# Issuing the stores of a softmax-gradient kernel from Pool in place of ACT

## The chip, the core and the metric

The kernel runs on one core of a Trainium2 chip. A core has a matrix engine (PE), a vector engine (DVE), a scalar engine (ACT), GpSimd (Pool) and a sync engine (SP), each with its own queue of instructions, and 16 DMA engines that all queues share. The metric is the device time of one execution in microseconds, as the median of several runs.

## What is computed

For each of 8 x 1024 = 8192 rows of 8192 float32 logits the kernel computes the softmax and subtracts one at the row's label. 268 MB come in and 268 MB go out.

```python
logits_max = np.max(logits, axis=-1, keepdims=True)
exp_logits = np.exp(logits - logits_max)
softmax = exp_logits / np.sum(exp_logits, axis=-1, keepdims=True)
...
one_hot[batch_idx, seq_idx, labels] = 1.0
return (softmax - one_hot).astype(np.float32)
```

## The kernel before

The 8192 rows are cut into 64 tiles of 128 rows (one row in each partition, 32 KB of it). Two tiles form a group, so there are 32 groups; within a group each partition holds two neighbouring rows, 64 KB. SBUF has three slots (`SLOTS`) of one group each, `X`, and everything is done in place in them: a tile is loaded into its slot, turned into its gradient there, and stored from there.

The order is written out by hand. `run` appends an instruction to an engine's queue, with the semaphore values it has to wait for, and returns the semaphore value that it will reach. Because every instruction is recorded in that helper, nearly all have line 68 in the profile, and the waits that are split off from them line 67.

- `load(b)` issues the loads of group `b` on SP. The string `LOADS` says how: "r" as two DMAs of one tile (4 MB), "w" as one DMA of both tiles (8 MB). A load into a slot that was used before waits for the stores from that slot to land (`put` semaphores). There are 43 loads: 22 of one tile, 21 of two.
- `row_max(t)` lets DVE take the negated maximum of each row of tile `t` into `m`; it waits for the load (`got` semaphores).
- ACT computes the exponential in place, with the row sum in `s`. DVE computes `r`, its reciprocal. ACT scales the row by `r`, in place. DVE subtracts one at the label: it compares an index row `iota`, which lies in PSUM as int16, with the label, and subtracts.
- `store(t)` issues the store of tile `t` (4 MB), after DVE's last step on that tile (`finished[t]`). All 64 stores are of this kind.

In the loop over tiles, DVE's queue holds the reciprocal of tile `t`, then the maximum of tile `t + 1`, then the subtraction of tile `t`. ACT's queue holds the exponential of tile `t`, then the store of tile `t - 1`, then the scaling of tile `t`. For the last tile the scaling and the subtraction are done in two halves. At the end, ACT waits for the stores of the last three groups. Pool only prepares: an identity matrix, and the index row, which it writes into the third slot before that is loaded.

Of the kernel before, what the change touches and what calls it, by code (L numbers as in the profile page):

```python
# [9 lines left out]
SLOTS = 3  # L10
# [7 lines left out]
def kernel(  # L18
# [6 lines left out]
    nc = tc.nc  # L25
# [30 lines left out]
    with tc.tile_critical():  # L56
        sem = tc.alloc_semaphore
        got = [[sem(f"got{i}{q}") for q in range(2)] for i in range(SLOTS)]
        put = [[sem(f"put{i}{q}") for q in range(2)] for i in range(SLOTS)]
# [3 lines left out]
        def run(engine, waits, counter, method, **operands):  # L63

            waits = list(dict.fromkeys(waits))
            for w in waits[:-1]:
                engine.wait_ge(*w)
            instruction = getattr(engine, method)(**operands)  # L68
            for w in waits[-1:]:
                instruction._wait_ge(*w)  # L70
            step = 16 if method == "dma_start" else 1
            instruction.then_inc(counter, step)
            count[counter.name] = count.get(counter.name, 0) + step
            return counter, count[counter.name]
# [3 lines left out]
        w = run(nc.gpsimd, [], pool, "memset", ap=ident[:], constant=0.0)  # L78
# [13 lines left out]
        for j in range(G):  # L92
            w = run(
                nc.tensor, [w_ident, w_lab], pe, "transpose",
                out=lab_ps[:, j, :], in_=lab_f[:, j, :], identity=ident[:],
            )
# [20 lines left out]
        loaded, stored, finished = {}, {}, []  # L117
# [14 lines left out]
        def store(t):  # L132
            b, j = divmod(t, G)
            stored.setdefault(b, [])
            for q, piece in enumerate(PIECES[STORES[b]]):
                ps, js = piece
                if js.stop != j + 1:
                    continue
                w = run(
                    nc.scalar, [finished[t]], put[b % SLOTS][q], "dma_start",  # L140
                    out=o_b[b, ps, js, :], in_=X[ps, b % SLOTS, js, :],
                )
                stored[b].append((piece, w))
# [16 lines left out]
        for t in range(T):  # L160
            x = row(t)
            label = lab[:, t % G, t // G : t // G + 1]
            w = run(
                nc.scalar, [w_max], act, "activation",
                out=x, in_=x, func=Act.Exp, bias=m[:, t : t + 1], scale=1.0, accum_out=s[:, t : t + 1],
            )
# [5 lines left out]
            if t > 0:  # L172
                store(t - 1)
# [10 lines left out]
            for c, w in zip(cols, scaled):  # L184
                w = run(
                    nc.vector, [w], dve, "scalar_tensor_tensor",
                    out=x[:, c], in0=iota[:, c], scalar=label, in1=x[:, c],
                    op0=Alu.is_equal, op1=Alu.subtract, reverse1=True,
                )
            finished.append(w)  # L190
        store(T - 1)
        for b in range(B - SLOTS, B):
            for _, w in stored[b]:
                nc.scalar.wait_ge(*w)


# [28 lines left out]
```

## Time and profile before

| what | value |
|---|---|
| time, median of 3 runs | 1247.4 us (1247.38 to 1247.5) |
| span of the profiled execution | 1245.7 us, 592 instructions |
| DVE, ACT, Pool busy | 1119.2, 919.1, 7.4 us |
| loads (SP's queue, q1) | 6192 packets, 268.44 MB |
| stores and the labels (ACT's queue, q10) | 9264 packets, 268.51 MB |
| mean DMA rate over the span | 431 GB/s |

The times come from the page of one profiled execution, the first row from the timed runs; of the profiled execution the page gives the span, from the first to the last instruction, which leaves out the start and end of the launch around it. A packet is one contiguous piece that a DMA engine moves; the last piece of each DMA on each engine is a mark of 4 bytes that raises the semaphore, which is why the queues have 16 small packets for each DMA besides their data. The queue q10 also carries the labels.

### The profile page before, as it was taken

The page shows a single profiled execution, that of the slowest core. Times are in us where ns is not written, and L with a number is a line of the kernel's source. Part 1 is how long each engine was busy: PE and PEld are TensorE (multiplying, and loading weights), DVE is VectorE, ACT ScalarE, POOL GpSimd, SP SyncE. Part 2 cuts the span into 40 slices and gives each one's busy share as a digit, 9 for nine tenths or more (in the row PEclk, how much of TensorE's full clock was granted, in tenths as well). Part 3 has the DMA queues.
Part 4 walks back from the last instruction along what each step waited for, and adds up shares of the span by engine and source line. Part 5 has one row for each costly group of instructions (what it writes and reads, how often), then busy time and mean ns, then how long its engine had stood idle before and what let it go on. Part 6 is the DMA issues. An engine that isn't in the chain of part 4 may idle for free.

```text
span 1245.7 us, 592 instructions
## 1 busy us (share of the span) xinstructions
PE 0.4 (0%) x2; PEld 0.3 (0%) x2; DVE 1119.2 (90%) x196; ACT 919.1 (74%) x194; POOL 7.4 (1%) x7
## 2 busy tenths in 40 slices
PE   0000000000000000000000000000000000000000
PEld 0000000000000000000000000000000000000000
DVE  5999998888988889888998888988889999999893
ACT  3888886778776787767877778777777788887772
POOL 2000000000000000000000000000000000000000
DMA  9999999999999999999999999999999999999998
GB/s 406 417 429 433 438 433 442 437 426 427 430 435 445 439 417 442 426 430 437 432 443 438 420 435 432 430 437 450 420 426 437 436 428 432 437 435 429 432 437 386
DMA packets 15460, 536.98 MB, mean 431 GB/s; under 512 B 1728, under 2 KB 1728, under 8 KB 1760
## 3 DMA queue, kind: packets, MB, share of 16 engines
q1 hardware_dynamic: 6192, 268.44, 50.0%
q10 hardware_dynamic: 9264, 268.51, 49.9%
q14 instruction: 4, 0.03, 0.0%
HBM read 268.50 MB, written 268.44 MB: 431 GB/s over the span
## 4 chain that ended last, share of the span: by engine, by line
DMA 59%; DVE 37%; another core or an unknown queue 2%; ACT 1%; DVEq 0%; issue 0%; PE 0%; SPq 0%; ACTq 0%
DMA X<-in_logits_dram 31%; DMA out_dram<-X 27%; DVE m L68 18%; DVE X L68 18%; ACT X L68 1%; DVE iota L68 0%; DVEq L56 0%; DMA lab_raw<-in_labels_dram 0%; DVE lab_f L68 0%; DVE r L68 0%; PE iota L68 0%; SPq L68 0%; ACTq L68 0%; DVE lab L68 0%
## 5 line engine op out<-in xcount | busy, mean ns | idle before, releaser
L68 DVE TENSOR_REDUCE m<-X 128x1 f32<-128x8192 f32 x64 | 555.2, 8675 | 94.3 <-DMA X<-in_logits_dram 94.3
L68 ACT ACTIVATE X<-X,m 128x8192 f32<-128x8192 f32 x64 | 455.9, 7123 | 188.4 <-DVE m L68 188.4
L68 DVE SCALAR_TENSOR_TENSOR X<-iota,lab,X 128x8192 f32<-128x8192 int16 (+1 forms) x65 | 559.7, 8612 | 4.1 <-ACT X L68 4.1
L68 ACT ACTIVATE X<-X,r 128x8192 f32<-128x8192 f32 (+1 forms) x65 | 456.0, 7017 | 115.9 <-DVE r L68 115.9
L68 DVE RECIPROCAL r<-s 128x1 f32<-128x1 f32 x64 | 9.9, 154 | 7.3 <-ACT X L68 7.3
L68 ACT ACTIVATION_READ_ACCUMULATOR X<-X,m 128x1 f32 x64 | 12.0, 187 | 0.0
L68 DVE CAST lab_f<-lab_raw 32x256 f32<-32x256 int32 x1 | 3.7, 3685 | 4.7 <-DMA lab_raw<-in_labels_dram 4.7
L68 POOL IOTA X<- 128x8192 int16 x1 | 6.9, 6944 | 0.0
L68 DVE TENSOR_SCALAR iota<-X 128x4096 int32<-128x4096 int32 x1 | 4.4, 4427 | 0.1
L68 ACT ACT_TABLE_LOAD x1 | 1.3, 1283 | 1.3 <-SPq L56 1.3
L68 DVE COPY lab<-iota 128x64 f32<-128x64 f32 x1 | 0.2, 225 | 0.5 <-PE iota L68 0.5
L68 PE MATMUL iota<-ident,lab_f 32*128 32x32 f32 x2 | 0.4, 300 | 8.5 <-DVE lab_f L68 8.5
L68 PEld LDWEIGHTS iota<-ident,lab_f 32*128 32x128 f32 x2 | 0.3, 196 | 8.4 <-DVE lab_f L68 8.4
L68 POOL TENSOR_SCALAR_AFFINE_SELECT ident<-ident 32x32 f32<-32x32 f32 x1 | 0.2, 204 | 0.1
L68 POOL MEMSET ident<- 32x32 f32 x1 | 0.1, 115 | 0.5 <-SPq L56 0.5
L209 POOL MEMSET const-bfloat16-1.0<- 128x1 bf16 x1 | 0.1, 107 | 0.0
L209 POOL MEMSET const-uint8-127<- 128x1 uint8 x1 | 0.1, 107 | 0.0
L209 POOL MEMSET const-float32-0.0<- 128x1 f32 x1 | 0.1, 104 | 0.2 <-issue 0.2
L209 POOL MEMSET const-float32-1.0<- 128x1 f32 x1 | 0.1, 104 | 0.0
## 6 DMA issues: line engine op xcount, KB each, us to landing
out_dram<-X ACTq DMA_DIRECT2D x64, 4096.0 KB, 30.8
X<-in_logits_dram SPq DMA_DIRECT2D x22, 4096.0 KB, 26.6
X<-in_logits_dram SPq DMA_DIRECT2D x21, 33.4
lab_raw<-in_labels_dram ACTq DMA_DIRECT2D x1, 64.0 KB, 3.8
```

The costliest lines, as they stand in the source:

```text
L68: instruction = getattr(engine, method)(**operands)
L209: nc = _bacc.Bacc("TRN2", target_bir_lowering=False, num_devices=1)
```

## The change

The 64 stores are issued from Pool's queue. The waits at the end of the program for the last six of them move with them. What each store waits for, what it moves, and their order among themselves stay as they are, and so do all loads and all compute instructions.

```diff
@@ -137,7 +137,7 @@
                 if js.stop != j + 1:
                     continue
                 w = run(
-                    nc.scalar, [finished[t]], put[b % SLOTS][q], "dma_start",
+                    nc.gpsimd, [finished[t]], put[b % SLOTS][q], "dma_start",
                     out=o_b[b, ps, js, :], in_=X[ps, b % SLOTS, js, :],
                 )
                 stored[b].append((piece, w))
@@ -191,7 +191,7 @@
         store(T - 1)
         for b in range(B - SLOTS, B):
             for _, w in stored[b]:
-                nc.scalar.wait_ge(*w)
+                nc.gpsimd.wait_ge(*w)
```

## The prediction

> **What bounds the kernel now.** I read the page's busy shares first, then its slices and DMA queues, then windows, waits and the last microseconds.
>
> ```profile
> span 1245.7 us, 592 instructions
> PE 0.4 (0%) x2; PEld 0.3 (0%) x2; DVE 1119.2 (90%) x196; ACT 919.1 (74%) x194; POOL 7.4 (1%) x7
> ...
> DMA  9999999999999999999999999999999999999998
> ...
> q1 hardware_dynamic: 6192, 268.44, 50.0%
> q10 hardware_dynamic: 9264, 268.51, 49.9%
> ```
>
> No compute engine is full: DVE 90%, ACT 74%, Pool almost empty. The DMA row is 9 in all slices but the last, and the two queues (q1: loads from SP, q10: stores from ACT) together fill 99.9% of the 16 DMA engines' time. A digit 9 could still hide 10% of idle time; the windows say it doesn't (the last two columns are DMA share and GB/s):
>
> ```profile
> 200.00:600.00 400.00, 0.00 (x0) 0.00 (x0) 358.66 (x64) 295.26 (x63) 0.00 (x0) 1.00 1.00 434
> 600.00:1000.00 400.00, 0.00 (x0) 0.00 (x0) 361.30 (x62) 299.66 (x63) 0.00 (x0) 1.00 1.00 433
> ...
> 1235.00:1240.00 5.00, 0.00 (x0) 0.00 (x0) 0.00 (x0) 0.00 (x0) 0.00 (x0) 1.00 0.99 426
> 1240.00:1245.70 5.70, 0.00 (x0) 0.00 (x0) 0.00 (x0) 0.00 (x0) 0.00 (x0) 1.00 0.41 178
> ```
>
> The share is 1.00 until about 1240 us. So the time is the sum of the packets' times on an engine. In the trace's records of single packets, one of 32,768 bytes takes 1.213 us and one of 65,536 bytes 2.418 us, nearly without spread. Per engine: stores 512 x 1.213 = 621 us; loads 168 x 2.418 + 176 x 1.22 (the first ones are slower) = 621 us; in all 1242 us. The engines start about 2 us into the span, the last store lands at 1244.15, and the waits and barriers behind it take 1.55 us.
>
> ```profile
> SPq L68 <- DMA out_dram<-X: 699.1, 37, 57.3
> SPq L67 <- DMA out_dram<-X: 446.9, 21, 21.5
> ...
> ACT X L68 <- DVE m L68: 188.4, 64, 19.7
> ...
> DVE m L68 <- DMA X<-in_logits_dram: 94.3, 25, 6.9
> ```
>
> These waits show who feeds whom: SP's loads wait for stores to land and free a slot, DVE's row maximum waits for loads, ACT for DVE. They alternate in the chain of waits too, which makes store latency look critical. But a 4 MB store lands a median 30.8 us after its issue only because it shares full engines with a load. What counts is whether the engines ever run dry. From issues and packet ends I added up the bytes issued but not moved: at the issue of each of the first 62 stores at least 8.4 us of work (at 431 GB/s) is still queued, at the 63rd 7.1 us, and at the last 3.6 us.
>
> ```profile
> 1217.03 0.15 DVE L68 RECIPROCAL r<-s 128x1 f32<-128x1 f32 x1
> 1217.14 0.34 ACTq L68 DMA_DIRECT2D out_dram<-X  x1
> 1217.53 7.31 ACT L68 ACTIVATE X<-X,r 128x4096 f32<-128x4096 f32 x2 [1.83 <-DVE r L68]
> 1221.27 8.88 DVE L68 SCALAR_TENSOR_TENSOR X<-iota,lab,X 128x4096 f32<-128x4096 int16 x2 [4.09 <-ACT X L68]
> 1230.18 0.34 ACTq L68 DMA_DIRECT2D out_dram<-X  x1
> ```
>
> This timeline is the end: row 62's store, row 63's scaling and subtraction, and the last store, issued 13.9 us before it lands.
>
> **The change part by part.** *ACT loses 64 issues of 338 ns, 21.6 us.* Each stands between two ACTIVATEs and starts when DVE has finished the row before. Without it the scaling ACTIVATE starts about 0.35 us earlier, but DVE's next step on that row waits for its own 8.68 us row maximum, against 7.12 us of scaling: 1.2 us of cover that was there already. Only for row 63 there is no maximum to hide behind, and there the last store could be issued 0.3 us earlier; queued packets cover that. Worth 0 us. ACT's waits on the last stores also leave; nothing is queued behind them but the end.
>
> *Pool gains 64 stores, each behind a wait for DVE's subtraction.* What is queued behind a waiting store on Pool is only the next store; Pool's 6.94 us index row ends at 8.3 us, and the first store is due at 47 us. Each store waits for the same DVE step as before, and in the same order, so SP's loads and the slots keep their releases. Loads stay on SP.
>
> *Start of a store.* No row shows Pool issuing a DMA. Below, it could be as quick as ACT's 0.34 us. Above, I use the whole trip of a small transfer on idle engines, the label load: 3.78 us from issue to landing; a path slower by that much again starts each store 3.8 us later. For 63 stores the queued work (7.1 us and more) covers both ends: 0. For the last store 3.6 us is queued on average, but the engines' end marks lie 2.1 us apart, so the emptiest has about 2.4 us: between 0 and 1.4 us exposed. I take 0.5.
>
> *The packets themselves.* The bytes and rows are the same; whether a packet from Pool's queue costs what one from ACT's does, the trace cannot show. The fixed part of a packet is 2 x 1213 - 2418 = 8 ns; shedding it wholly saves 512 x 8 = 4.1 us per engine, the bound below zero. Cutting each 32 KB row into four packets of 8 KB adds 3 x 8 ns to each: +12.3 us, the bound above. Nearest is the one other kind of queue in the trace, the instruction fetch (q14): its 8,192-byte packets have a median of 311.5 ns where the two rows above give 309.3. I take that 2.2 ns: 512 x 2.2 ns = +1.1 us.
>
> *The end.* Pool now waits for the last stores and then runs its DRAIN, in front of the last barrier. Before, Pool's DRAIN there took 41 ns, with no DMA of Pool's to account for; DVE's, with a step still running, took 5.3 us until it was over. If Pool settles its 64 stores one by one at the end, the price is 64 times something: nothing at the low end; at the high end what ACT pays to issue one, 64 x 0.338 = 21.6 us. Nearest is Pool's own DMA bookkeeping instruction in the preamble (INC_SWDGE_SEM, 27 ns): 64 x 27 ns = +1.7 us, which I take.
>
> **A rule against the change.** DVE's two long steps take 8,675 and 8,612 ns for 8,192 elements per partition, 1.06 and 1.05 ns each, and the subtraction reads one operand from PSUM; no long step runs at a faster rate. The Trainium skill ("SBUF — State Buffer", "Who interferes with whom") says that a DMA issued from GpSimd can't write its descriptors while VectorE runs in a two-port mode. By it as it stands nothing is blocked here, since it exempts a reduction and steps with one SBUF input; if it bit anyway, the sum would be that of the late start below. The skill ("DMA: Bandwidth & Descriptors", "Latency and other measured facts") also says that DMA engines 7 and 15 are usually slower, with descriptor rings of GpSimd's DMAs as a guess. It gives no figure, and no run here shows it; the packets of this trace hardly spread, so my sum goes without it.
>
> **Sum.** 0 + 0.5 + 1.1 + 1.7 = +3.3 us on the span of 1245.7. The profile gives its execution only as that span; the three timed runs have a median of 1247.4, 1.7 us more for what lies around it, and I keep that: 1247.4 + 3.3 = 1250.7 us.
>
> **The rivals.** *No measurable difference.* The packets cost the same, the last store's start is covered, Pool's drain is as short as now: 1247.4, up to 1248. For it speaks the full DMA row, which hides everything before 1230 us. About 0.2% (2.5 us) is what a measurement of this kernel can tell from no change; this ends within it.
>
> *Faster.* One mechanism: packets from Pool's queue lose their fixed 8 ns on the engines, in all 512 store packets of each: 1243.3. It decides from 4.9 ns per packet (2.5 us / 512). Against it: both queues shown pay the fixed part.
>
> *Slower packets.* They are cut finer, or some engines serve Pool's queue slower; every transfer uses all 16 engines, so the slowest sets the pace. In four pieces: 1247.4 + 12.3 + 2.2 = 1262. Each further 1% on the stores' 621 us is 6 us.
>
> *Late starts.* If each issue waits until DVE's running step is over (8.7 us), the covers of 8.4 to 9.5 us run short. With a start 10 us late, the 64 shortfalls add up to 24 us, with one 8.8 us late to 7.5; so 1255 to 1271. Against it: no sign in the rows that Pool and DVE hinder each other; Pool's index row ran while DVE hardly worked.
>
> **How the numbers follow.** Forecast (an end of Pool's that costs, packets about equal; own range 1250 to 1256) 0.46; no difference 0.24; faster 0.12; slower packets 0.12; late starts 0.06. Slower by over 0.2%: 0.46 + 0.12 + 0.06 = 0.64; same 0.24; faster 0.12. The range reaches to the faster rival's value and past the four-piece case, 1243 to 1264; outside lie the higher half of the slower packets, most late starts above 1264 and a drain near its upper bound, some 0.15.
>
> **What would show it.** Right: a third queue with 8192 data packets and the same share as q10 now, a DMA share of 1.00 until about 1240 us, no ACT issues, and 1 to 5 us more between the last store's issue and the end. Wrong: another packet count or share of that queue (packets), a DMA share under 1.00 in the middle (late starts), a span shorter than 1244 (fixed part shed), or an end as short as 1.55 us after the last landing (no drain cost).

## The result and the profile after

The changed kernel takes 1254.36 us (median of 4 runs, 1252.78 to 1256.18), beside 1247.45 for the kernel before on the same chip (median of 4: three within 0.12 us, one at 1251.61): a ratio of 1.0052, 95% interval 1.0034 to 1.0069. It is slower by about half a per cent. The profiled execution, the fastest of the four, took 1252.78 us, with a span of 1251.0: 5.3 us more than the span before.

The page of the changed kernel, the rows that answer to those shown before:

```profile
span 1251.0 us, 592 instructions
PE 0.4 (0%) x2; PEld 0.3 (0%) x2; DVE 1116.6 (89%) x196; ACT 919.0 (73%) x194; POOL 41.6 (3%) x71
...
DMA  9999999999999999999999999999999999999997
...
q1 hardware_dynamic: 6192, 268.44, 49.8%
q0 software_dynamic: 9216, 268.44, 49.7%
q10 hardware_dynamic: 48, 0.07, 0.0%
```

The stores are in a queue of their own now, q0, of another kind. Its 9216 packets are 8192 of data and 64 x 16 end marks, as many as the stores had on q10. Their shares are those of before, for a span that is longer by 0.4%. Windows of the changed kernel (DMA share and GB/s in the last two columns):

```profile
200.00:600.00 400.00, 0.00 (x0) 0.00 (x0) 358.53 (x64) 295.72 (x63) 11.16 (x21) 1.00 1.00 433
600.00:1000.00 400.00, 0.00 (x0) 0.00 (x0) 359.69 (x62) 297.68 (x62) 10.64 (x20) 1.00 1.00 433
1235.00:1240.00 5.00, 0.00 (x0) 0.00 (x0) 0.00 (x0) 0.00 (x0) 0.00 (x0) 1.00 1.00 433
1240.00:1245.00 5.00, 0.00 (x0) 0.00 (x0) 0.00 (x0) 0.00 (x0) 0.00 (x0) 1.00 0.62 269
1245.00:1251.00 6.00, 0.00 (x0) 0.00 (x0) 0.00 (x0) 0.00 (x0) 0.00 (x0) 1.00 0.00 0
```

Up to the last landing no time is lost in this profile: the engines are full, at 433 GB/s, and the last store lands at 1244.16 us, where it landed before. Then six microseconds pass in which no engine computes and nothing moves. Who holds the end is to be read from the waits in SP's own queue, in the rows of line 56, the end of the hand-ordered block (us in total, times, longest). Before, SP's last wait there was the following, for ACT, which awaited the last stores:

```profile
SPq L56 <- ACTq L56: 14.5, 1, 14.5
```

After, it is for Pool, and longer by 4.6 us although the last issue is 0.9 us later:

```profile
SPq L56 <- POOLq L56: 19.1, 1, 19.1
```

The views leave out semaphore and DRAIN instructions, but the trace has them; a DRAIN is an instruction that the trace shows on each of these engines at the end of the block. Pool sees the last store's semaphore and starts its DRAIN at 1244.77 us; that takes 5.292 us. Pool's DRAIN before the change took 0.041 us, and lay at 1173.5 us, with no DMA of Pool's in the kernel; behind the last landing stood ACT's, of 0.008. The difference, 5.25 us (5.28 against ACT's), is the whole difference of the two spans. That Pool settles its stores there one by one is the theory that the experiments test.

The issue itself, in the view of the stores' instructions, before and in the changed kernel (min/median/max ns):

```profile
L68 ACTq DMA_DIRECT2D out_dram<-X x64: 338/338/363, 47.0 to 1230.2; - x64
...
L68 POOL DMA_DIRECT2D out_dram<-X x64: 531/531/673, 47.3 to 1231.1; - x64
...
DMA to landing us min/median/max: 13.4/30.3/50.7
```

It takes 531 ns on Pool for 338 on ACT; 63 of the 64 took 531 or 533 ns, whatever DVE was doing, and the first one 673. ACT lost its 64 issues without a gain, as its waits show, one row from before and two from the changed kernel:

```profile
ACT X L68 <- DVE r L68: 115.9, 64, 2.1
...
ACT X L68 <- DVE m L68: 209.5, 64, 19.6
ACT X L68 <- DVE r L68: 95.6, 64, 1.5
```

It waits 20.3 us less in front of the scaling and 21.1 us more in front of the next exponential (188.4 before, shown above).

### The profile page after: what moved, and what is told of

The parts are those of the page before. It is cut to its first block, busy times and chain, and to the rows that moved or that the text cites. A ratio compares the mean times of both kernels' runs of the same rounds, so it can differ in the third digit from the quotient of the medians.

```text
span 1251.0 us, 592 instructions
## 1 busy us (share of the span) xinstructions
PE 0.4 (0%) x2; PEld 0.3 (0%) x2; DVE 1116.6 (89%) x196; ACT 919.0 (73%) x194; POOL 41.6 (3%) x71
## 3 DMA queue, kind: packets, MB, share of 16 engines
q0 software_dynamic: 9216, 268.44, 49.7%
## 4 chain that ended last, share of the span: by engine, by line
DMA 59%; DVE 37%; issue 1%; ACT 1%; POOL 0%; PE 0%; ACTq 0%; DVEq 0%; POOLq 0%; SPq 0%
DMA X<-in_logits_dram 32%; DMA out_dram<-X 27%; DVE m L68 19%; DVE X L68 18%; ACT X L68 1%; DMA lab_raw<-in_labels_dram 1%; DVE iota L68 0%; DVE r L68 0%; DVE lab_f L68 0%; POOL out_dram L68 0%; PE iota L68 0%; DVE lab L68 0%; ACTq L220 0%; DVEq L67 0%; POOLq L194 0%
## 5 line engine op out<-in xcount | busy, mean ns | idle before, releaser
L68 POOL DMA_DIRECT2D out_dram<-X x64 | 34.2, 534 | 1189.1 <-DVE r L68 1177.0
L68 DVE CAST lab_f<-lab_raw 32x256 f32<-32x256 int32 x1 | 1.1, 1121 | 7.3 <-DMA lab_raw<-in_labels_dram 7.3
## 6 DMA issues: line engine op xcount, KB each, us to landing
out_dram<-X POOLq DMA_DIRECT2D x64, 4096.0 KB, 30.3
```

## The experiments

Theories: **settling** (Pool's DRAIN accounts for the DMAs that Pool issued, so much for each, and the end waits for that; the word is a name for the cost, and what Pool does in that time no trace shows); **fixed cost** (having used Pool's queue costs some 5 us once); **last stores** (the time is the landing or receipt of the last stores, seen from Pool); **slower packets** (the cost is spread over the run).

### The changed kernel again, and its two halves

First, the changed kernel unaltered.

> The changed kernel once more, unaltered, to have it beside the others on one chip. In its first profile Pool's DRAIN, between the last landing and the barrier, took 5.29 us; before the change 0.04 us. All theories: span about 1251, DRAIN 5.2 to 5.4 us, last landing at 1244 us, time 1252.5 to 1254.5.

Measured: 1254.75 us (5 runs, 1253.8 to 1256.2) beside 1247.59 before, ratio 1.0058 (1.0046 to 1.0070). DRAIN 5.292 us again. The time is a little above the 1254.5 that I had allowed. In this profile the last landing is at 1245.18, 1 us later than in the first. The median is above before by 7.2 us, of which the DRAIN is 5.25; some 1.9 us are left. This profile, of the fastest of the five runs, shows 1.0 of them, ahead of the last landing.

Then the waits alone on Pool:

```diff
-                nc.scalar.wait_ge(*w)
+                nc.gpsimd.wait_ge(*w)
```

> The other half alone: stores on ACT as before the change, only the waits for the last six on Pool. Theory 'settling': Pool has no store of its own, so its DRAIN after the waits is 0.03 to 0.2 us, the time that of before within 0.5 us. Rival 'Pool's waits are slow' (waiting on Pool at the end costs the 5 us whoever issued): 1252 to 1253.

Measured: 1247.60 us (11 runs), ratio 1.0000 (0.9991 to 1.0008); DRAIN 0.041 us. Waiting on Pool costs nothing that these runs can tell.

And the stores alone on Pool, with the waits on ACT (the first hunk of the change without the second):

> All 64 stores stay on Pool; only the waits for the last six go back to ACT, so that Pool's DRAIN starts at about 1231.6 us, right after its last issue, while stores are still landing. Theory 'settling' (the DRAIN accounts for Pool's stores one by one, some 82 ns each, and can do so for those that have landed while the rest still move): the DRAIN is long, 12 to 13 us, but ends within 0.5 us of the last landing at 1244.2, and the time is that of before within 1 us (1247 to 1248.5). Rival 'after the last landing' (a cost of about 5.3 us that begins only when the last store has landed): DRAIN ends at 1249.5, time 1252.5 to 1254 as for the changed kernel. Rival 'ACT's waits are quicker than Pool's': the same gain without a DRAIN that overlaps the landings; the DRAIN would again be 5.3 us long.

Measured: 1251.99 us (5 runs), ratio 1.0043 (1.0031 to 1.0055), 2.8 us less than the changed kernel. Settling had promised the time of before, and about half of the DRAIN's 5.25 us came. The waits in SP's queue of this kernel show why:

```profile
SPq L56 <- ACTq L56: 14.8, 1, 14.8
...
SPq L56 <- POOLq L56: 2.4, 1, 2.4
```

ACT's wait is about as long as before the change, and Pool still comes 2.4 us after it. Its DRAIN ran beside the last landings for 17.04 us, and ended 3.0 us after the last store had landed (at 1250.37 us: the profile is that of the slowest of the five runs, 1256.08 us). So 3.0 us stay behind the last landing, 3.0 us / 64 stores = 47 ns each. Whether the rest was done ahead of it, or a DRAIN that has begun early is quicker afterwards, is not shown. My expectation of "within 0.5 us" was wrong.

### How the DRAIN grows

Which stores Pool issues, by tile; the other engine's stores get semaphores of their own (their allocation is left out here):

```diff
+                engine, landed = (nc.gpsimd, put) if t % 2 else (nc.scalar, put_act)
                 w = run(
-                    nc.gpsimd, [finished[t]], put[b % SLOTS][q], "dma_start",
+                    engine, [finished[t]], landed[b % SLOTS][q], "dma_start",
```

> Odd tiles' stores on Pool, even ones' on ACT (semaphores of their own); the waits for the odd ones of the last groups on Pool. 32 stores of Pool's in place of 64. Theory 'settling, per store': Pool's DRAIN takes 32 x 82 ns = 2.6 us. Rival 'fixed cost of having used Pool's queue': 5.3 us. Rival 'something about the last stores alone': 5.3 us.

With `t >= 56` in the condition:

> Only the stores of tiles 56 to 63 on Pool, the other 56 on ACT; waits for the last ones on Pool. Theory 'settling, per store': Pool's DRAIN takes 8 x 82 ns = 0.66 us. Rival 'fixed cost' or 'the last stores alone': 5.3 us, since the same last stores are issued and awaited by Pool as in the changed kernel.

Every store in two DMAs of 64 partitions each:

```diff
+                for h in range(2):
+                    c = slice(h * P // 2, (h + 1) * P // 2)
                     w = run(
                         nc.gpsimd, [finished[t]], put[b % SLOTS][q], "dma_start",
-                    out=o_b[b, ps, js, :], in_=X[ps, b % SLOTS, js, :],
+                        out=o_b[b, c, js, :], in_=X[c, b % SLOTS, js, :],
                     )
```

> Every store cut into two DMAs of 64 partitions each, both on Pool: 128 DMAs, but the same 8192 data packets of 32,768 bytes, and 128 x 16 marks in place of 64 x 16. If the DRAIN's cost goes by DMA: 128 x 82 ns = 10.5 us. If it goes by packets (data and marks, on each engine 128 x 5 = 640 for 64 x 9 = 576): 5.9 us. If fixed: 5.3 us.

And a DRAIN in the middle:

```diff
             finished.append(w)
+            if t == 40:
+                nc.gpsimd.drain()
```

> The changed kernel with one more DRAIN on Pool, after the issue of store 39 and ahead of store 40. Theory 'settling': the DRAIN at the end has only 24 stores left, 24 x 82 ns = 2.0 us. The added one shows whether a DRAIN holds Pool until its stores have landed: then it takes as long as store 39's landing, 15 to 35 us, stores 40 and 41 start late, and the time may be longer for that; if it only accounts for landed ones, 3 us or less. Rival 'fixed cost' or 'last stores alone': the DRAIN at the end is 5.3 us.

Of these four kernels there is one run each. With them and the runs below, the last DRAIN by the number of Pool's DMAs since the one before it, where all of them had landed when it began:

| Pool's DMAs | 0 | 8 | 24 | 32 | 43 | 56 | 64 | 128 |
|---|---|---|---|---|---|---|---|---|
| DRAIN, us | 0.041 | 0.709 | 2.014 | 2.674 | 3.577 | 4.634 | 5.292 | 10.514 |

That is a straight line: (10.514 - 0.709) / 120 = 81.7 ns for each DMA, and some 0.05 us besides. The 128 halves decide between DMAs and packets: by packets they would have cost 5.9 us. Bytes are out as well: 43, 64 and 128 DMAs moved the same 268 MB. Fixed cost and last stores are out: with the last eight stores issued and awaited by Pool the DRAIN is 0.71 us.

The DRAIN in the middle took 28.8 us, from the issue of store 39 until 2.05 us after that store had landed at 817.68 us (40 stores, 51 ns each, next to the 47 above). Pool was held meanwhile, as this timeline of that kernel shows:

```profile
808.11 7.12 ACT L68 ACTIVATE X<-X,r 128x8192 f32<-128x8192 f32 x1 [1.51 <-DVE r L68]
...
820.25 0.53 POOL L68 DMA_DIRECT2D out_dram<-X  x1 [28.72 <-issue]
```

Store 40 could go when the scaling of the next tile began, near 808 us, and went at 820.25, 12 us late. Its time, 1253.8 us, is no longer than the changed kernel's for that: the DRAIN at the end is 3.3 us shorter, the last landing 4.3 us later (1248.46).

### Out of the end's way

Stores 0 to 55 on Pool, the last eight and the waits on ACT (the lines around this one as for the odd tiles above):

```diff
+                engine, landed = (nc.gpsimd, put) if t < 56 else (nc.scalar, put_act)
```

> Stores 0 to 55 on Pool, 56 to 63 on ACT (with semaphores of their own), the waits at the end on ACT. Theory 'settling': Pool's DRAIN runs while ACT's last stores are still being issued and moved, so nothing of it is in front of the barrier: time of before within 1 us, DRAIN over before 1200 us. Rival 'packets from Pool's queue are slower' (a cost spread over the whole run): 56/64 of the 5.3 us stay, about 1252.

Measured: 1263.0 us (6 runs, 1258.8 to 1275.6), ratio 1.0157 (1.0115 to 1.0199). The DRAIN was over at 1170 us, as expected, and yet this is worse than the changed kernel. The end of it, in windows of the kernel before (the first row) and of this one:

```profile
1226.00:1236.00 10.00, 0.00 (x0) 0.00 (x0) 4.15 (x1) 0.00 (x0) 0.00 (x0) 1.00 1.03 446
...
1217.00:1226.00 9.00, 0.00 (x0) 0.00 (x0) 7.65 (x1) 6.88 (x1) 0.00 (x0) 1.00 1.04 448
1226.00:1236.00 10.00, 0.00 (x0) 0.00 (x0) 9.76 (x3) 7.21 (x2) 0.00 (x0) 1.00 0.09 39
1236.00:1246.00 10.00, 0.00 (x0) 0.00 (x0) 6.15 (x2) 7.31 (x2) 0.00 (x0) 1.00 0.98 419
```

and the row maximum of the last tile in the timelines of both (the helper is line 69 here):

```profile
1199.76 8.69 DVE L68 TENSOR_REDUCE m<-X 128x1 f32<-128x8192 f32 x1 [1.93 <-DMA X<-in_logits_dram]
...
1218.35 8.69 DVE L69 TENSOR_REDUCE m<-X 128x1 f32<-128x8192 f32 x1 [1.94 <-DMA X<-in_logits_dram]
```

The last load lands 18.6 us later than before the change, all queued stores are gone by then, and the engines are empty (share 0.09) while the last tile is computed. After the switch two queues of stores stand beside the one of loads, and the loads get less of the engines and fall behind. The single packets of the two traces show it: from 1115 to 1140 us Pool's stores held 0.36 of the engines, ACT's 0.33 and the loads 0.31, where the loads had 0.49 before the change. Over 1090 to 1150 us the loads lost 5.6 us of the engines' time. At 1199.4 us, where the last load had landed before, they had 8.0 us of it still to take, and at the share of 0.43 that they got this lasted the 18.6 us. The two kernels with mixed stores above agree: their last maximum starts at 1212.9 us (eight stores on Pool, 1258.3 us) and 1250.0 (odd ones, 1298.2 us); in the first the loads held 0.35 from 1110 to 1145 us, before the change 0.51. The Trainium skill ("DMA: Bandwidth & Descriptors", "Issuing engines are not separate DMA queues") says that transfers from all issuing engines interleave on the same 16 DMA engines, and that issuing from several only saves issue time. The runs agree that nothing was gained; what they add is that with two queues of stores in place of one the loads' share fell from about a half to about a third here, and with it the last load came later.

The other way to move Pool's DMAs away from the end is to give it loads:

```diff
+                engine, landed = (nc.sync, got) if b < SLOTS else (nc.gpsimd, got_pool)
                 w = run(
-                    nc.sync, free, got[b % SLOTS][q], "dma_start",
+                    engine, free, landed[b % SLOTS][q], "dma_start",
```

> Stores and waits stay on ACT as before the change; the loads of groups 3 to 31 move to Pool (37 DMAs), with semaphores of their own, and SP keeps the first six. Pool's last load is issued near 1173 us and lands near 1200 us, 45 us before the last store, so its DRAIN (37 x 81.6 ns + 0.07 = 3.1 us) has no part in the end. Theory 'the DRAIN is the cost, and only its place at the end': time of before within 0.5 us, 1247 to 1248. Theory 'Pool's queue also disturbs the engines' (the 1.9 us by which the changed kernel's median is above before plus DRAIN): 1248.5 to 1251, the last load landing later than 1200 us. Theory 'whatever is issued by Pool pays at the end': 1250.5.

Measured: 1248.98 us (12 runs), ratio 1.0014 (1.0006 to 1.0023). The DRAIN ended at 1209.4 us, 1.9 us after Pool's last load had landed, and has no part in the end. So most of the loss is gone with it. What is left, 1.1 us, is more than the 0.5 us of the first theory and lies at the lower end of the second's range: Pool as the issuer of many DMAs cost a little besides its DRAIN, and by what is not shown. In the one profile, that of the longest of these runs (1254.47 us), the last load lands 8 us later than before the change.

### Wide stores

If the DRAIN goes by DMAs, fewer and larger stores should help:

```diff
-STORES = "rrrrrrrrrrrrrrrrrrrrrrrrrrrrrrrr"
+STORES = "rrrrrwwwwwwwwwwwwwwwwwwwwwrrrrrr"
```

> As the changed kernel, but 21 of the 32 groups (those loaded by one DMA) are also stored by one DMA of 8 MB: 43 stores on Pool in place of 64, the bytes the same, packets of 65,536 bytes in their place. Theory 'settling, per DMA': Pool's DRAIN takes 43 x 81.6 ns + 0.07 = 3.6 us, 1.7 us less than with 64. If it went by bytes it would stay 5.3. The packets' fixed part falls by 21 x 8 x 8 ns = 1.4 us per engine, so the time is 1250 to 1253 if the engines stay full; against that the first tile of a group now waits for the second before it is stored, and engines that run dry for it could eat all of it.

> The same wide stores on ACT. No DRAIN of Pool's to pay. If the engines stay full, 1.4 us less than before: 1246; if the later stores let them run dry, longer. The difference from the same stores on Pool is 3.5 us by the DRAIN, plus the 1 to 2 us by which the last load landed later in profiles with Pool's stores, if that comes from Pool's queue.

Measured: 1343.9 us on Pool (ratio 1.0781, 1.0763 to 1.0799) and 1345.7 on ACT (1.0790, 1.0776 to 1.0804). The DRAIN is 3.577 us as expected, and the two profiled spans differ by about that (1341.0 and 1337.2, each of the fastest run); the medians don't, as the runs scatter over 7.5 and 9.1 us. But both kernels lose 92 to 98 us elsewhere. Windows of the one on ACT:

```profile
300.00:700.00 400.00, 0.00 (x0) 0.00 (x0) 322.44 (x57) 266.12 (x57) 0.00 (x0) 1.00 0.96 397
700.00:1100.00 400.00, 0.00 (x0) 0.00 (x0) 333.84 (x59) 275.84 (x58) 0.00 (x0) 1.00 0.95 395
```

The share is 0.95, no longer 1.00: the engines do run dry, as expected of a first tile that waits for the second of its group, though no run separates that wait. Over the whole span this is some 54 us more than before. The rest is in the loads' packets: those of 65,536 bytes take a mean of 2.63 us for 2.42 before, and the loads' packets together 38 us more on each engine. I had saved 1.4 us on paper and named the risk without a price; the risk was seventy times as large.

## Why the prediction was right, and where its sum was off

The direction and the mechanism held: slower, by an end on Pool that costs, with the packets about equal. 1254.36 us lies in the forecast's own range of 1250 to 1256; the point, 1250.7, was 3.7 us too low. The signs named for it came too: 8192 data packets in a third queue, a share of 1.00 until about 1240 us, no issues on ACT, and 4.4 us more from the last store's issue to the end.

- *What bounds it:* right. With whole-tile stores on one queue the engines are full to about 1215 us in the profiles (but for the DRAIN in the middle, which let some 2 us go), and in both of the changed kernel to the end; the work queued hid all that happened before.
- *ACT's 64 issues, worth 0:* right; 20 us went from one wait to another.
- *Start of the last store, +0.5:* the first packet came 2.52 us after the issue began, before the change 2.41; exposed 0.
- *Packets, +1.1:* the median is 1.213 us on Pool's queue too; the sum of all packets' time per engine rose by 0.7 us, in the loads. The 2.2 ns that I took from the instruction fetch's packets did not appear in Pool's.
- *The end, +1.7:* the mis-sized term. 64 x 27 ns should have been 64 x 81.7 ns = 5.2 us. The form (so much for each store, after the last landing) was right; the row chosen for the price, one bookkeeping instruction, was no price for it and three times too low. The 41 ns set beside it were of a DRAIN at 1173.5 us, not at the end; the waits alone on Pool show that, with no DMA of Pool's, it takes as long there.
- *What the sum lacked:* the 1.7 to 1.9 us by which the medians exceed before plus DRAIN, in runs that scatter over 3.4 and 2.4 us (17 runs of before: 1.9). In the two profiles of the changed kernel the last load is later: the last maximum starts at 1200.7 and 1202.0 us, before at 1199.8. But in the profile of the waits alone on Pool, whose DMAs all come from SP and ACT, it starts at 1202.8 (its longest run, 1249.36 us), so a late last load needs no DMA of Pool's. In the medians, stores on Pool and loads on Pool are slower by more than their DRAIN, and waits on Pool are not. What these 1 to 2 us are is open.
- *Luck:* the 0.5 and 1.1 us that did not come nearly make up for the 1.7 to 1.9 that were not in the sum. That the point missed by little more than the 3.5 us by which the end was mis-sized is owed to that.
- *Late starts behind DVE:* did not happen; 531 ns at the minimum and at the median, with DVE at 89%, and a store lands a median 30.3 us after its issue, before 30.8. So the exemption for such DVE steps in the Trainium skill ("SBUF — State Buffer", "Who interferes with whom") fits this trace.
- *Slower engines 7 and 15*, which the Trainium skill reports ("DMA: Bandwidth & Descriptors", "Latency and other measured facts"), do not show in the packets' times: of the 8192 data packets of Pool's queue 49 took more than 1.214 us, where two engines of 16 move 1024.

## What to carry to other kernels

Where DMA engines are full from start to end, as here, moving a whole stream's issue to another engine gained nothing in the middle; look at what the new issuer still has to do after the last landing, and who waits for it. With Pool as the issuer of all stores, its DRAIN stood in front of the end at 81.7 ns for each DMA, so Pool should not be the issuer of many transfers up to the very end. The price was out of the way where Pool's last DMA came early (56 stores, or the loads), and by all but 24 stores where a DRAIN of its own stood in the middle, though that kernel was no faster; early stores alone do not do it, as all 64 were paid at the end. Don't split one stream of stores over two queues, or join stores into larger ones, without asking when the last load will land: from there the last tile's own chain, 41 to 44 us here (57 with the stores in halves), runs to the last landing.

## What I had not expected of the hardware

Pool's DRAIN took 81.7 ns for each DMA that Pool had issued since the DRAIN before, whatever the DMA's size (4 or 8 MB, or 2 MB halves). Where it started early it held Pool until its last DMA had landed, and then needed some 50 ns for each of them still (47 for 64 DMAs, 51 for 40, 52 for 37); these three points would fit a fixed part with a smaller price for each as well.

Stores cut into halves of 64 partitions take 1457.4 us, 210 more than before, of which the DRAIN is 10.5; the store packets are of the same 32,768 bytes, at a mean of 1.49 us and 5.5 at most, for 1.213. The Trainium skill ("SBUF — State Buffer", "Door 1: The DMA port swizzle") says that partitions 0 to 63 reach only 8 of the 16 ports; packets of which some take much longer, with a median still at 1.213, agree with that, though no run here looked at ports.
